# Eight second-layer modulation blocks moved from the attention stage to the first part of the RWKV mixer

## The chip, the cores and the metric

The kernel runs on one core of a Trainium2 chip. The metric is the time of one execution on the device, in microseconds (us). The time of the kernel before is the median of three runs. Beside it stands one profiled execution, whose trace gives every duration and wait that is used below. A change of 0.5%, which is 11.4 us here, is about what a measurement of this kernel can tell from no change.

## What is computed

Two layers of a diffusion backbone work on 512 latent tokens and 256 context tokens of width 1024. Layer 0 mixes the tokens with grouped-query attention, layer 1 with a two-directional RWKV-7 recurrence, and a dense SwiGLU follows each. All of it is modulated: six vectors of 1024 per layer (shift, scale and gate, for the mixer and for the SwiGLU) come from the conditioning vector `c` for the latents and from `c_ctx` for the context.

```python
for i in range(DEPTH):                                   # two layers
    m  = (silu(c)     @ mod_w[i] + mod_b[i]).reshape(B, 6, 1, D)
    mc = (silu(c_ctx) @ mod_w[i] + mod_b[i]).reshape(6, D)
    h  = rmsnorm(x,  norm1_g[i]) * (1 + m[:, 1]) + m[:, 0]
    hc = rmsnorm(xc, norm1_g[i]) * (1 + mc[1])   + mc[0]
    y, yc = attention(h, hc) if i == 0 else rwkv7(h, hc)
    x  = x + m[:, 2] * y
    h2 = rmsnorm(x, norm2_g[i]) * (1 + m[:, 4]) + m[:, 3]
    x  = x + m[:, 5] * swiglu(h2)
    ...                                                  # the context likewise, in layer 0 only
return rmsnorm(x, final_g)
```

`mod_w[i]` is a float32 matrix of 1024 x 6144. Of layer 1's six vectors only `m[:, 0]` and `m[:, 1]` (and `mc[0]`, `mc[1]`) are wanted at the RWKV mixer's entry. `m[:, 2]` is first wanted after the scan, at the output projection, and `m[:, 3]` to `m[:, 5]` later still.

## The kernel before

Activations lie with the model width on the 128 partitions: `xT[p, k, t]` holds feature 128 k + p of token t, for eight values of k and 768 tokens. Most products split both float32 operands into a high and a low float32r part and take three matmuls for the one product.

**A modulation block.** `mod_block` (L117 to L138) computes 512 of the 6144 columns for both conditioning vectors at once; a layer has twelve blocks, j = 0 to 11, two for each of the six vectors. It loads its weights, 1024 x 512 float32 or 2 MB, into tiles `mw`; eight float32 matmuls follow, one for each 128 rows. They use 32 columns of the array each, so row block k goes to column quarter k mod 4, and four of them are issued in a row. ScalarE copies the result out of PSUM (`mev`, L128), four small matmuls against `sel` add the quarters and bring the features to the partitions (L131), and VectorE adds the bias into `modT` (L132). `mod_scale` (L139 on) makes `aT`, the scale times the norm's gain, from `modT` and `par1`. The inputs of all blocks, `sc` (the silu of `c` and `c_ctx`) and `par1` (biases and gains), are in a pool that is closed when layer 0's SwiGLU opens its own.

**Stages, in the order of the trace.** Loading, norm and the first four blocks of layer 0 end at about 60 us; the q, k, v projections run to about 176 us. Then comes attention: the program lists twenty blocks (j = 4 to 23, that is the rest of layer 0 and all of layer 1) ahead of the loop over heads, each block with two weight tiles of 1 MB from two buffers. The loop over eight pairs of heads follows, for the latents first and then for the context; for each tile of 128 queries there are score matmuls `S` (L728), a maximum on VectorE (L731), an exponential on ScalarE (L735), transposes `PTp` (L742) with copies out, and for each pair the products `po` (L747). Next are the output projection and the SwiGLU of layer 0 (L228, L395, L445), whose end is layer 1's norm (`norm_stream`, L521 and L522).

The first part of the RWKV mixer starts there, at about 1026 us. `shift` builds `xx`; `lerp` builds eight tiles of `u + xx * mix[j]` on VectorE (`lt`, L897), casts them on ScalarE (`lh`, L899) and subtracts on VectorE or GpSimd (`ll`, L901), in a ring of 13 tiles; `dense(2, ...)` is the k projection, four column groups b whose weights `wraw` come in four loads of 256 KB each (L217), are cast to `whi` and subtracted to `wlo`. `sink_k` stores each result and sums squares through a tile `kq` into `ssk` (L936). Three narrow products (`rwkv_w1`, `rwkv_g1`, `rwkv_a1`) follow with a lerp each, then the normalisation of k (L991, L993, whose output `kkt` also takes the `kq` buffers), the lerp for v, and stores of the lerp for r (`d_rl`). The v projection (L1220 to L1222) and the scan come after.

**What sets the order.** The program is written for a framework that sets all semaphores and reorders: at compile time a planner runs through the program with planned durations and gives each engine's queue its order. Earlier lines of the program go first where several instructions are ready; an instruction that isn't ready lets later ones pass. On the chip each queue then runs in the planned order, and an instruction that has to wait holds up all behind it on its queue. Nearly all loads and stores are issued by SP, so SP's queue is one such order.

Of the kernel before, what the change touches and what calls it, by code (L numbers as in the profile page):

```python
# [10 lines left out]
F32 = mybir.dt.float32  # L11
# [6 lines left out]
P = 128  # L18
D = 1024
KT = D // P  # L20
L = 512
C = 256
T = L + C
# [14 lines left out]
def tile_hybrid_backbone(ctx: ExitStack, tc: tile.TileContext, a: dict, out: bass.AP, dbg=None, stop=None, start=None):  # L38
# [33 lines left out]
    with tc.tile_pool(name="prm", bufs=1, side="right", reuse_waits="tile") as prm, \  # L72
            tc.tile_pool(name="prm_ps", bufs=1, space=PSUM, reuse_waits="tile") as pps:
        rawc = prm.tile([2 * KT, P], F32, name="rawc")
        nc.scalar.dma_start(out=rawc[0:KT], in_=a["c"].rearrange("l (r p) -> (l r) p", p=P))
        nc.scalar.dma_start(out=rawc[KT:2 * KT], in_=a["c_ctx"].rearrange("(r p) -> r p", p=P))
        ps = pps.tile([P, P], F32, name="psc", tag="ps")
        nc.tensor.transpose(ps[:, 0:2 * KT], rawc, ident[0:2 * KT, 0:2 * KT])
        nc.gpsimd.memset(sc, 0.0)
        for s in range(2):  # L80
            nc.scalar.activation(sc[:, :, s], ps[:, 8 * s:8 * s + 8], AF.Silu)
        raw1 = prm.tile([P, P], F32, name="raw1")
        row = 0
        for name, n in (("mod_b", 96), ("norm1_g", 16), ("norm2_g", 16)):
            nc.scalar.dma_start(out=raw1[row:row + n, :], in_=a[name].rearrange("l (r p) -> (l r) p", p=P))
            row += n
        ps = pps.tile([P, P], F32, name="ps1", tag="ps")
        nc.tensor.transpose(ps, raw1, ident)
        nc.vector.tensor_copy(par1, ps)

    def mixer_params(prm, pps, tag):
        raw2 = prm.tile([96 + 8, P], F32, name="raw2")
# [17 lines left out]
        nc.vector.tensor_copy(par2, ps[:, 0:row])  # L110
        nc.vector.tensor_copy(ln.rearrange("p x f -> p (x f)"), ps[:, 256:256 + 2 * KT])

    modb = par1[:, 0:96].rearrange("p (l j) -> p l j", l=2)
    norm_g = par1[:, 96:128].rearrange("p (w l f) -> p w l f", w=2, l=2)


    def mod_block(pool, pspool, l, j, bufs=2, npc=2, tags=("aux", "aux"), pbufs=None):  # L117
        ps = pspool.tile([P, 512], F32, name="mps", tag=tags[0], bufs=pbufs)
        v = a["mod_w"][l].rearrange("(k p) f -> p k f", p=P)[:, :, 512 * j:512 * (j + 1)]
        nk = KT // npc  # L120
        for i in range(npc):
            w = pool.tile([P, nk, 512], F32, name="mw", tag="mw", bufs=bufs)
            nc.sync.dma_start(out=w, in_=v[:, nk * i:nk * i + nk, :])
            for k in range(nk * i, nk * i + nk):
                g = k % 4
                nc.tensor.matmul(ps[32 * g:32 * g + 32, :], sc[:, k, :], w[:, k - nk * i, :], start=(k < 4), stop=(k >= 4))  # L126
        ev = pool.tile([P, 512], F32, name="mev", tag="mev", bufs=1)
        nc.scalar.copy(ev, ps)  # L128
        ps2 = pspool.tile([P, 512], F32, name="mps2", tag=tags[1], bufs=pbufs if tags[0] == tags[1] else None)
        for q in range(4):  # L130
            nc.tensor.matmul(ps2[:, 2 * q:2 * q + 2], ev[:, 128 * q:128 * q + 128], sel, start=True, stop=True)  # L131
        nc.vector.tensor_tensor(  # L132
            out=modT[:, l, 4 * j:4 * j + 4, :],
            in0=ps2[:, 0:8].rearrange("p (q s) -> p q s", s=2),
            in1=modb[:, l, 4 * j:4 * j + 4].unsqueeze(2).to_broadcast([P, 4, 2]),
            op=ALU.add,
        )

    def mod_scale(l, w, half):  # L139
        m = (1, 4)[w]  # L140
        ks = slice(4 * half, 4 * half + 4)
        nc.vector.scalar_tensor_tensor(
            out=aT[:, 2 * l + w, ks],
            in0=modT[:, l, 8 * m + 4 * half:8 * m + 4 * half + 4, :],
            scalar=1.0,
            in1=norm_g[:, w, l, ks].unsqueeze(2).to_broadcast([P, 4, 2]),
            op0=ALU.add,
            op1=ALU.mult,
        )
# [375 lines left out]
    def layer0():  # L525
# [168 lines left out]
        with ExitStack() as sm:  # L694
# [3 lines left out]
            pst = pool(sm, "pst", 2, psum=True)  # L698
            pso = pool(sm, "pso", 1, psum=True)
            psa = pool(sm, "psa", 1, psum=True)  # L700
            for j in range(4, 24):
                mod_block(md, psa, j // 12, j % 12)

            ready = {}
            for b in range(2):
                raw = md.tile([P, KT, 256], F32, name="mw", tag="mw", bufs=2)
                nc.sync.dma_start(out=raw, in_=a["attn_wo"][0].rearrange("(k p) f -> p k f", p=P)[:, :, 256 * b:256 * b + 256])
                ready[b] = [raw[:, 0:4], raw[:, 4:8]]
            for l, w in ((0, 1), (1, 0), (1, 1)):
                for half in range(2):  # L710
                    mod_scale(l, w, half)
            tap("modT", modT[:, 0])
# [73 lines left out]
    else:  # L786
        xTs[0] = pool(xs, "xT").tile([P, KT, T], F32, name="xT")
        nc.sync.dma_start(out=xTs[0], in_=a["x0"])
        with ExitStack() as ms:
            md = pool(ms, "md")  # L790
            pam = pool(ms, "pam", 2, psum=True)
            mixer_params(md, pam, "aux")
            for j in range(12):
                mod_block(md, pam, 1, j)
            for w in range(2):
                for half in range(2):
                    mod_scale(1, w, half)
            for s, _, _ in ORDERED:
                norm_stream(s, md, pam.tile([P, 512], F32, name="rbc", tag="aux"))
        mods.close()  # L800
# [9 lines left out]
    with ExitStack() as rw:  # L810
# [37 lines left out]
        with ExitStack() as de:  # L848
# [13 lines left out]
            hkk = up.tile([P, KT], F32, name="hkk")  # L862
            xx = pool(de, "xxp").tile([P, KT, T], F32, name="xx")
            pk = pool(de, "pk", 1, psum=True)


            def shift(k, s, off, w):
# [68 lines left out]
                    nc.tensor.matmul(ssk[:, i, f, :], sq[:, P * i:P * i + P], h2, start=True, stop=True)  # L936

            dense(2, 1, T, sink_k, True)

            hbf = ep.tile([P, T], F32, name="hb", tag="lt")[:, 0:384]  # L940
            hb = hbf.rearrange("p (f h) -> p f h", f=KT)
# [545 lines left out]
```

## Time and profile before

| | |
|---|---|
| median of three runs | 2289.47 us (2286.93 to 2295.59) |
| profiled execution | 2281.48 us, of which the trace spans 2279.8 us |
| PE busy | 2024.0 us, 89% of the span |
| DVE busy | 1694.4 us, 74% |
| ACT busy | 1128.5 us, 49% |
| POOL busy | 787.6 us, 35% |
| granted TensorE clock, mean | 0.93 |
| loads of `mod_w` | 48 of 1024 KB, 5.3 us from issue to landing |

The profiled execution is one run. It is 8.0 us shorter than the median and 5.5 us shorter than the fastest of the three, so a difference between two profiles isn't the difference of two medians. PE is TensorE's matmuls and PEld its weight loads, DVE is VectorE, ACT ScalarE, POOL GpSimd and SP the queue that issues DMAs. A busy share is a mean over all stages; what a stage is limited by is read in the stage. "Granted clock" is the share of full speed that TensorE was given.

### The profile page before, as it was taken

What the parts mean: (1) busy time and instruction counts of PE and PEld (TensorE: products, weight loads), DVE (VectorE), ACT (ScalarE), POOL (GpSimd) and SP (SyncE); (2) the same over time, 40 slices, a digit from 0 to 9 for tenths busy, and PEclk for the clock granted to TensorE, in tenths of its full rate; (3) what the DMA queues carried; (4) which work ended last, traced back from release to release, by engine and by line L of the source; (5) the groups of instructions that cost most, each with busy time, mean ns of one, the idle gap of its engine ahead of it and who ended that gap; (6) DMA issues with size and microseconds to landing.
All of it is one profiled execution on the core that took longest, in us unless ns stands there. A gap on an engine that the chain in (4) does not pass through costs nothing.

```text
span 2279.8 us, 43273 instructions
## 1 busy us (share of the span) xinstructions
PE 2024.0 (89%) x16566; PEld 1785.4 (78%) x16566; DVE 1694.4 (74%) x3439; ACT 1128.5 (49%) x2338; POOL 787.6 (35%) x642
## 2 busy tenths in 40 slices
PE   6999999898999999994988877778778777999998
PEld 4995555797999999994858855667667667899998
DVE  4565555669677777669385598799787778899997
ACT  5446566655333333336243754765654556444443
POOL 1110000136444344413142532543330325666661
PEclk8999999999999999997978988878888978999999
DMA  8206772443222221211344543433321654433332
GB/s 301 67 22 221 236 234 73 147 149 137 68 61 70 74 75 56 74 54 59 101 153 153 161 132 107 116 85 94 91 59 32 187 179 120 147 99 96 111 94 74
DMA packets 196445, 260.56 MB, mean 114 GB/s; under 512 B 17384, under 2 KB 129232, under 8 KB 195856
## 3 DMA queue, kind: packets, MB, share of 16 engines
q1 hardware_dynamic: 195520, 256.95, 36.2%
q8 instruction: 131, 2.15, 0.4%
q10 hardware_dynamic: 352, 0.60, 0.1%
q14 instruction: 74, 0.61, 0.1%
q0 software_dynamic: 368, 0.26, 0.1%
HBM read 211.62 MB, written 33.55 MB: 108 GB/s over the span
## 4 chain that ended last, share of the span: by engine, by line
PE 63%; DVE 21%; DMA 5%; ACT 4%; issue 4%; POOL 2%; SPq 0%; DVEq 0%; POOLq 0%; ACTq 0%
PE yps L445 13%; PE A L395 8%; PE B L395 5%; PE C L395 5%; PE yps L228 5%; DVE O L1167 3%; PE po L747 3%; PE S L728 2%; PE pj L228 2%; DVE E L1170 2%; PE PTp L742 2%; PE mps L126 2%; PE qps L595 2%; PE qps L597 2%; PE qps L596 2%
## 5 line engine op out<-in xcount | busy, mean ns | idle before, releaser
L445 PE MATMUL yps<-gh,wu 128*128 128x384 f32 (+2 forms) x1120 | 324.4, 345 | 0.0
L258 DVE SCALAR_TENSOR_TENSOR xT<-yps,modT,xT 128x384 f32<-128x384 f32 (+3 forms) x360 | 185.2, 537 | 124.7 <-PE yps L445 105.9
L239 ACT CAST wu<-wr 128x512 fp32r<-128x512 f32 x276 | 168.5, 619 | 171.6 <-PE A L395 56.6
L239 ACT CAST wu<-ws 128x512 fp32r<-128x512 f32 x176 | 109.1, 621 | 222.6 <-PE yps L445 66.4
L445 PEld LDWEIGHTS yps<-gh,wu 128*128 128x128 f32 x1120 | 202.7, 189 | 11.4
L241 POOL TENSOR_TENSOR wu<-wr,wu 128x512 fp32r<-128x512 f32 x86 | 123.8, 1439 | 241.2 <-ACT wu L239 217.6
L445 PE MATMUL yps<-gl,wu 128*128 128x384 f32 (+2 forms) x560 | 193.2, 345 | 0.0
L349 POOL TENSOR_TENSOR ws<-wr 128x512 f32<-128x512 f32 x88 | 130.0, 1482 | 141.8 <-DMA wr<-in_ffn_wg_dram 56.4
L241 DVE TENSOR_TENSOR wu<-wr,wu 128x512 fp32r<-128x512 f32 x190 | 161.8, 857 | 12.9 <-ACT wu L239 12.4
L241 DVE TENSOR_TENSOR wu<-ws,wu 128x512 fp32r<-128x512 f32 x111 | 135.5, 1221 | 22.2 <-ACT wu L239 22.0
L241 POOL TENSOR_TENSOR wu<-ws,wu 128x512 fp32r<-128x512 f32 x65 | 100.1, 1540 | 66.1 <-ACT wu L239 65.9
L228 PE MATMUL yps<-oTh,wu 128*128 128x384 f32 (+1 forms) x512 | 110.9, 309 | 1.1 <-ACT wu L239 1.0
L445 PEld LDWEIGHTS yps<-gl,wu 128*128 128x128 f32 x560 | 105.8, 189 | 4.3
L731 DVE TENSOR_REDUCE mx<-S 128x1 f32<-128x768 f32 (+1 forms) x96 | 74.7, 778 | 44.2 <-PE S L728 43.6
L395 PE MATMUL C<-x5h,wu 128*128 128x384 f32 (+1 forms) x352 | 85.0, 319 | 14.5 <-ACT x5h L312 12.3
L743 ACT COPY PT<-PTp 128x384 f32<-128x384 f32 (+1 forms) x160 | 69.4, 466 | 53.8 <-PE PTp L742 53.6
L241 POOL TENSOR_TENSOR wu<-mw,wu 128x512 fp32r<-128x512 f32 x2 | 2.9, 1458 | 263.9 <-ACT wu L239 263.9
L742 PEld LDWEIGHTS PTp<-ident,pr 128*128 128x128 f32 x448 | 50.2, 144 | 50.4 <-issue 23.6
L1167 DVE TENSOR_TENSOR O<-E 128x110 f32<-128x110 f32 (+22 forms) x288 | 87.9, 341 | 2.2
L395 PE MATMUL A<-x1h,wu 128*128 128x384 f32 (+1 forms) x352 | 83.1, 311 | 4.5 <-POOL wu L241 2.1
L228 PEld LDWEIGHTS yps<-oTh,wu 128*128 128x128 f32 x512 | 85.4, 189 | 1.9 <-ACT wu L239 1.4
L395 PE MATMUL B<-x2h,wu 128*128 128x384 f32 (+1 forms) x352 | 84.5, 309 | 0.2 <-POOL wu L241 0.2
(409 smaller groups left out, 6482.7 us busy)
## 6 DMA issues: line engine op xcount, KB each, us to landing
mw<-in_mod_w_dram SPq DMA_DIRECT2D x48, 1024.0 KB, 5.3
wr<-in_ffn_wg_dram SPq DMA_DIRECT2D x44, 512.0 KB, 4.1
wr<-in_ffn_wu_dram SPq DMA_DIRECT2D x44, 512.0 KB, 3.8
wr<-in_ffn_wd_dram SPq DMA_DIRECT2D x44, 512.0 KB, 3.9
wraw<-in_rwkv_wrkv_dram SPq DMA_DIRECT2D x32, 256.0 KB, 3.2
wr<-in_rwkv_wo_dram SPq DMA_DIRECT2D x16, 512.0 KB, 4.7
wraw<-in_attn_wqkv_dram SPq DMA_DIRECT2D x12, 512.0 KB, 4.8
xT<-xd SPq DMA_DIRECT2D x2, 3072.0 KB, 11.0
```

The source lines that it names most:

```text
L228: nc.tensor.matmul(ps, w(k), x(k, sl), start=(k == 0 and i == 0), stop=(k == nk - 1 and i == 2))
L239: nc.scalar.copy(hi, raw)
L241: (nc.gpsimd if lane["n"] % 3 == 0 else nc.vector).tensor_tensor(out=lo, in0=raw, in1=hi, op=ALU.subtract)
L258: nc.vector.scalar_tensor_tensor(out=xT[:, f, t0:t1], in0=ps[:, t0 - sl.start:t1 - sl.start], scalar=modT[:, l, 8 * m + f, s:s + 1], in1=x ...
L349: nc.gpsimd.tensor_tensor(out=t, in0=x, in1=y, op=op)
L395: nc.tensor.matmul(ps, w[:, k], x[:, k], start=(k + j == 0), stop=(k == 3 and j == 2))
L445: nc.tensor.matmul(ps, u[k // 2][w][:, k % 2, fs], gs[k // 2][x][:, k % 2, sl], start=(k + j == 0), stop=(k == nk - 1 and j == 2))
L731: nc.vector.tensor_reduce(out=mx, in_=S[:, :nk * P], axis=AX.X, op=ALU.max)
L742: nc.tensor.transpose(ps[:, t - t0, :], pr_[:, P * t:P * t + P], ident)
L743: nc.scalar.copy(PT[h][:, t0:t1, P * qt:P * qt + P], ps[:, :t1 - t0, :])
L747: nc.tensor.matmul(po[HD * h:HD * h + HD, :], vt[:, k0 // P + t, HD * kv:HD * kv + HD], PT[h][:, t, :], start=(t == 0), stop=(t == nk - 1))
L1167: nc.vector.tensor_tensor(out=tv, in0=E[:, a_:b, s:s + 1].to_broadcast([P, b - a_, m]), in1=E[:, s:s + 1, :s].to_broadcast([P, b - a_, m]) ...
```

## The change

Blocks j = 4 to 11 of layer 1, and the `mod_scale` of its second norm, are no longer listed before the loop over heads. They are listed behind `dense(2, 1, T, sink_k, True)` in the RWKV mixer. As the tiles `sc` and `par1` are gone by then, both are stored to DRAM at the start (two DMAs issued by ScalarE) and loaded again (two DMAs issued by SP). The moved blocks load their weights in eight pieces of 256 KB, one for each 128 rows, from three buffers in the pool `nm`; they use two PSUM banks of their own (`pm`) and a `kq` buffer for `mev`. The other twelve blocks of the attention stage stay as they are.

```diff
+    d_sc = dram.tile([P, KT, 32], F32, name="d_sc")
+    d_par = dram.tile([P, P], F32, name="d_par")
+    nc.scalar.dma_start(out=d_sc, in_=sc)
+    nc.scalar.dma_start(out=d_par, in_=par1)
...
-    def mod_block(pool, pspool, l, j, bufs=2, npc=2, tags=("aux", "aux"), pbufs=None):
+    mod_in = {"sc": sc, "par": par1}
+
+    def mod_block(pool, pspool, l, j, bufs=2, npc=2, tags=("aux", "aux"), pbufs=None, ev=None):
+        sc = mod_in["sc"]
+        modb = mod_in["par"][:, 0:96].rearrange("p (l j) -> p l j", l=2)
...
-        ev = pool.tile([P, 512], F32, name="mev", tag="mev", bufs=1)
+        ev = (ev or (lambda: pool.tile([P, 512], F32, name="mev", tag="mev", bufs=1)))()
...
-            for j in range(4, 24):
+            for j in range(4, 16):
                 mod_block(md, psa, j // 12, j % 12)
...
-            for l, w in ((0, 1), (1, 0), (1, 1)):
+            for l, w in ((0, 1), (1, 0)):
                 for half in range(2):
                     mod_scale(l, w, half)
...
             pk = pool(de, "pk", 1, psum=True)
+            pm = pool(de, "pm", 2, psum=True)
...
             dense(2, 1, T, sink_k, True)
+
+            sc2 = nm.tile([P, KT, 32], F32, name="sc2")
+            par2_ = nm.tile([P, P], F32, name="par1")
+            nc.sync.dma_start(out=sc2, in_=d_sc)
+            nc.sync.dma_start(out=par2_, in_=d_par)
+            mod_in.update(sc=sc2, par=par2_)
+            for j in range(4, 12):
+                mod_block(nm, pm, 1, j, bufs=3, npc=8, ev=lambda: ep.tile([P, T], F32, name="mev", tag="kq")[:, :512])
+            for half in range(2):
+                mod_scale(1, 1, half)
```

More of the change, by code (lines that the diff above doesn't have):

```diff
@@ L111, in mixer_params @@
         nc.vector.tensor_copy(ln.rearrange("p x f -> p (x f)"), ps[:, 256:256 + 2 * KT])
-    modb = par1[:, 0:96].rearrange("p (l j) -> p l j", l=2)
-    norm_g = par1[:, 96:128].rearrange("p (w l f) -> p w l f", w=2, l=2)
-    def mod_block(pool, pspool, l, j, bufs=2, npc=2, tags=("aux", "aux"), pbufs=None):
+    mod_in = {"sc": sc, "par": par1}
+    def mod_block(pool, pspool, l, j, bufs=2, npc=2, tags=("aux", "aux"), pbufs=None, ev=None):
+        sc = mod_in["sc"]
+        modb = mod_in["par"][:, 0:96].rearrange("p (l j) -> p l j", l=2)
         ps = pspool.tile([P, 512], F32, name="mps", tag=tags[0], bufs=pbufs)
@@ L140, in mod_scale @@
         m = (1, 4)[w]
+        norm_g = mod_in["par"][:, 96:128].rearrange("p (w l f) -> p w l f", w=2, l=2)
         ks = slice(4 * half, 4 * half + 4)
@@ L792, in tile_hybrid_backbone @@
             mixer_params(md, pam, "aux")
-            for j in range(12):
+            for j in range(4):
                 mod_block(md, pam, 1, j)
-            for w in range(2):
-                for half in range(2):
-                    mod_scale(1, w, half)
+            for half in range(2):
+                mod_scale(1, 0, half)
             for s, _, _ in ORDERED:
@@ L938, in tile_hybrid_backbone @@
             dense(2, 1, T, sink_k, True)
+            sc2 = nm.tile([P, KT, 32], F32, name="sc2")
[5 more added lines that the diff above has]
+                mod_block(nm, pm, 1, j, bufs=3, npc=8, ev=lambda: ep.tile([P, T], F32, name="mev", tag="kq")[:, :512])
+            for half in range(2):
+                mod_scale(1, 1, half)
             hbf = ep.tile([P, T], F32, name="hb", tag="lt")[:, 0:384]
```

## The prediction

> **What bounds the kernel now.** I read the busy times and the chain by line first, on the page, and then the chain within the attention stage alone.
>
> ```profile
> PE 2024.0 (89%) x16566; PEld 1785.4 (78%) x16566; DVE 1694.4 (74%) x3439; ACT 1128.5 (49%) x2338; POOL 787.6 (35%) x642
> PE yps L445 13%; PE A L395 8%; PE B L395 5%; PE C L395 5%; PE yps L228 5%; DVE O L1167 3%; PE po L747 3%; PE S L728 2%; PE pj L228 2%; DVE E L1170 2%; PE PTp L742 2%; PE mps L126 2%; PE qps L595 2%; PE qps L597 2%; PE qps L596 2%
> by line: PE po L747 24.2%; PE PTp L742 23.8%; PE S L728 21.4%; PE mps L126 21.2%; PE mps L131 8.8%; ACT pr L735 0.5%; ACT PT L743 0.3%; issue 0.0%
> ```
>
> The third line is the chain from 200 to 360 us. The blocks' matmuls (L126, L131) are 30% of it, and everything else in it is matmul too: attention is limited by PE, and the blocks are on its path. How much they take is read from windows that each begin at a pair's `po`, which is one pair of heads per row (span, then PE, PEld, DVE, ACT, POOL busy; clock, DMA share, GB/s):
>
> ```profile
> 204.63:231.86 27.23, 27.23 (x181) 15.42 (x177) 13.80 (x38) 15.84 (x35) 0.00 (x0) 1.00 0.69 231
> ...
> 313.58:340.82 27.24, 27.24 (x178) 15.46 (x177) 14.72 (x38) 16.25 (x37) 0.00 (x0) 1.00 0.71 233
> 340.82:364.65 23.83, 23.68 (x146) 14.17 (x145) 14.16 (x35) 15.17 (x36) 0.00 (x0) 1.00 0.56 182
> 364.65:382.99 18.34, 17.82 (x97) 10.50 (x96) 12.28 (x34) 12.63 (x33) 0.00 (x0) 1.00 0.00 0
> ```
>
> Five pairs take 27.24 us each with PE busy throughout; the last row holds no block and takes 18.34. The same windows for L126 and then for L131 alone (weight loads) tell how many blocks lie in them:
>
> ```profile
> 204.63:231.86 27.23, 0.94 (x48) 1.00 0.69 231
> 340.82:364.65 23.83, 0.47 (x24) 1.00 0.56 182
> ...
> 204.63:231.86 27.23, 2.92 (x24) 1.00 0.69 231
> 340.82:364.65 23.83, 1.95 (x16) 1.00 0.56 182
> ```
>
> At 16 records of L126 and 8 of L131 a block, a full pair carries three. Now the part that receives the blocks, in seven windows from the norm to the scan's start:
>
> ```profile
> 1026.55:1042.84 16.29, 3.80 (x22) 3.42 (x22) 15.61 (x44) 12.00 (x24) 6.53 (x12) 0.58 0.28 97
> 1042.84:1060.75 17.91, 10.58 (x47) 9.69 (x48) 16.93 (x30) 11.09 (x23) 11.04 (x8) 0.52 0.18 59
> 1060.75:1079.99 19.24, 12.84 (x52) 8.68 (x50) 17.85 (x25) 9.72 (x16) 0.86 (x5) 1.00 0.01 1
> 1079.99:1142.97 62.98, 61.15 (x372) 54.70 (x373) 21.76 (x26) 17.15 (x24) 9.17 (x5) 0.97 0.32 101
> 1142.97:1168.00 25.03, 20.77 (x103) 15.37 (x102) 21.82 (x26) 13.97 (x21) 8.67 (x7) 0.89 0.23 67
> 1168.00:1197.00 29.00, 23.29 (x66) 15.46 (x64) 25.92 (x22) 11.05 (x14) 14.33 (x8) 0.56 0.75 245
> 1197.00:1240.00 43.00, 35.75 (x249) 34.22 (x249) 22.14 (x26) 12.93 (x27) 9.13 (x10) 0.86 0.55 177
> ```
>
> It is three different stages. Norm and first lerps (to 1080 us) are limited by VectorE, 50.4 of 53.4 us, and PE has gaps. The k projection (1080 to 1143) is PE's, 61.15 of 62.98. From 1143 to 1197 VectorE is busy 47.7 of 54 us, and PE runs partly at half clock.
>
> **The change part by part.** *Out of attention.* The step from one PE group to the next gives a block's price:
>
> ```profile
> 332.38 1.07 PE L126 MATMUL mps<-mw,sc 128*32 128x512 f32 x8
> 333.38 0.87 PE L742 MATMUL PTp<-ident,pr 128*128 128x128 f32 x6
> ...
> 337.35 0.95 PE L131 MATMUL mps<-sel,mev 128*128 128x2 f32 x8
> 338.15 0.85 PE L742 MATMUL PTp<-ident,pr 128*128 128x128 f32 x6
> ...
> 200.00:360.00 160.00, 53.29 (x416) 22.89 (x416) 2.85 (x18) 10.61 (x18) 1.00 0.71 236
> ```
>
> Half a block holds PE for 1.00 us and its gather for 0.80, so a block is 2 x 1.00 + 0.80 = 2.80 us. By the chain it is 30% of 160 us for 18 blocks (the last row is that window for the tile `mps`, with 18 bias additions on DVE), 2.67; by the windows (27.24 - 18.34) / 3 = 2.97, though the last window has shorter context scores in it, and the pair at 340.82, less one and a half blocks of L126 and two of L131 (4.6 us), leaves 19.2, which makes (27.24 - 19.2) / 3 = 2.68. I take 2.78: 8 x 2.78 = 22.2 us less, between 21.4 and 23.7. Nothing else there becomes late: ACT's busiest pair is 16.25 and DVE's 14.72, both under 18.34.
>
> *At the start* two stores are issued on ACT's queue. An issue on SP costs 0.37 us (first row below), taken for ACT's also: 0.7 us. The store of `par1` must wait for its copy on DVE, and what is queued behind it on ACT, the squares of the input, waits with it. If the order puts it early, that is up to the 7.5 us that DVE itself waits there; I take 0.7, as the plan orders by readiness.
>
> ```profile
> L123 SPq DMA_DIRECT2D mw<-in_mod_w_dram x48: 367/368/2626, 5.8 to 348.1; - x48
> DVE par L89 <- PE ps L88: 7.5, 1, 7.5
> L128 ACT COPY mev<-mps x24: 563/587/598, 22.8 to 355.0; 128x512 f32<-128x512 f32 x24
> L132 DVE TENSOR_TENSOR modT<-mps,par x24: 148/156/167, 26.2 to 357.3; 128x8 f32<-128x8 f32 x24
> L142 DVE SCALAR_TENSOR_TENSOR aT<-modT,par x8: 152/166/169, 36.3 to 338.7; 128x8 f32<-128x8 f32 x8
> ...
> 1178.66 1.01 DVE L993 SCALAR_TENSOR_TENSOR kkt<-kt,hkk,pj 128x768 f32<-128x768 f32 x1 [0.32 <-PE pj L991]
> L998 DVE SCALAR_TENSOR_TENSOR lt<-xx,par,xT x8: 739/746/751, 1207.5 to 1225.0; 128x512 f32<-128x512 f32 x8
> ```
>
> *VectorE in the mixer*: 8 x 0.156 + 2 x 0.166 = 1.6 us, on the engine that limits two of the three stages. All of it counts: +1.6. *ScalarE*: 8 x 0.587 = 4.7 us. It has room in every window, but the lerps pass through it (`lt`, `lh`), and a copy that is running cannot be put off: a third counts, +1.5, between 0 and 4.7. The copies take `kq` buffers that the squares and `kkt` use too; `kkt` is 1.01 us of work in several, so this costs nothing while the ring turns, and a copy's length each time if not.
>
> *PE in the mixer.* A half block is cheap because four column quarters run at once. A piece of one row block that arrives alone has no partner. What a pass of 512 columns takes when few share is shown by `po`, whose halves load weights in pairs (start, us):
>
> ```profile
> 205.11 0.14 PEld L747 LDWEIGHTS po<-PT,vt 128*64 128x64 f32 x2 [0.28 <-issue]
> 205.54 0.14 PEld L747 LDWEIGHTS po<-PT,vt 128*64 128x64 f32 x2 [0.28 <-issue]
> ```
>
> 0.43 us a pass, two passes a float32 matmul: 0.86 us for a lone piece. The 64 pieces and eight gathers are 64 x 0.86 + 6.4 = 61.4 us if all are alone; three buffers let three share at best, 64 / 3 x 1.00 + 6.4 = 27.7. PE's gaps are 53.4 - 27.2 = 26.2 us up to 1080, 54.0 - 44.1 = 10.0 from 1143 to 1197 and 7.2 after, 43.5 in all. The middle of 27.7 and 61.4, 44.6, just fits. In between, from 1080 to 1143, there is no room, but the dense matmuls are earlier lines and go first; I count five lone pieces that slip in, +4, between 0 and the whole overflow, 61.4 - 43.5 = 17.9. Behind 1143 the blocks are the earlier lines and hold up the narrow products; VectorE has `kkt` and the `d_rl` tiles (L998, which stood at the end) to do meanwhile, 8 x 1.01 and 8 x 0.746 us. That is the cover, and without it the products' delay is the overflow just named.
>
> *SP and the weights.* The pieces pass SP's queue, 66 issues more, amid `wraw`, `d_k` and `kt`. A piece's issue waits until PE is done with the piece three before; a `wraw` load behind it waits too, then `whi`, `wlo` and the products. These stops exist already (total, times, longest; the three stages in turn):
>
> ```profile
> ACT whi L218 <- DMA wraw<-in_rwkv_wrkv_dram: 3.8, 3, 1.8
> ...
> ACT whi L218 <- DMA wraw<-in_rwkv_wrkv_dram: 5.2, 2, 3.5
> ...
> ACT whi L218 <- DMA wraw<-in_rwkv_wrkv_dram: 5.8, 4, 4.5
> ...
> wraw<-in_rwkv_wrkv_dram SPq DMA_DIRECT2D x30, 256.0 KB, 3.4
> ```
>
> A load of this size lands in 3.4 us, and two weight buffers cover most of it: +2.5, less than one landing, between 0 and 20 (six late loads). Three in flight in 3.4 us is 231 GB/s, and the first three windows move at most 97, so the wires have room. At that pace 64 pieces take 64 / 3 x 3.4 = 73 us, longer than the 53 to 1080: some three blocks fall behind 1143.
>
> The Trainium skill, DMA: Bandwidth & Descriptors (Rules for kernel authors), speaks against the edit: at least 1 MiB per DMA, where these are a quarter. Its fixed cost of 2.0 us plus bytes over 436 GB/s (Anatomy of one DMA, for GpSimd's path) would be an estimate of 2.6 us a piece, 55 us for all, and fewer blocks behind 1143; the 3.4 us measured decides.
>
> *The clock.* From 1168 to 1185 the chain is PE at 0.56 of its clock. First and last of its four stretches of `pj` (30 matmuls, 10.3 us), one of four `L991` steps (3.7 us in all), and the same matmuls at full clock:
>
> ```profile
> 1101.56 8.44 PE pj L228 x48
> ...
> 1168.04 3.84 PE pj L228 x12
> ...
> 1180.84 0.94 PE pj L991 x2
> 1181.78 2.22 PE pj L228 x6
> ```
>
> At 8.44 / 48 = 0.176 us the 30 would be 5.3 us, so 5.0 less, and half of the `L991` steps 1.9: up to 6.9 us back if the blocks keep PE awake there, nothing if they are over by then. I take 3.0. The Trainium skill, TensorE: Matmul & The Clock Gate (What's actually happening), says that activity releases the throttle; the trace agrees (0.52 and 0.56 where PE has gaps, 1.00 in attention), and by that rule alone the term would be the whole 6.9 and the sum 3.9 us lower.
>
> *Memory.* `nm` grows by 7.5 KB a partition (`sc2` 1, `par1` 0.5, three pieces of 2), so `xx` moves and waits for other tiles of the SwiGLU. Nothing, as `xx` needs the norm anyway; a late tile would cost what it is late.
>
> *Sum*: -22.2 + 0.7 + 1.6 + 1.5 + 4 + 2.5 - 3.0 = -14.9 us. The profiled execution, 2281.48, would be 2266.6; that execution lies 8.0 under the median, so the same difference goes on the median: 2289.47 - 14.9 = 2274.6, faster by 0.65%, with 2262 to 2283 as this case's own range. A measurement tells 0.5%, 11.4 us, from no change.
>
> **The rivals.** *No change to measure*: the pieces come one by one, each takes its 0.86 us, PE becomes the limit of the whole receiving part, and the clock gains nothing as the chain moves elsewhere. Then the PE term is 17.9: -22.2 + 0.7 + 1.6 + 1.5 + 17.9 + 2.5 = +2.0, or 2291.5. For it: one load per row block and only three buffers. Against it: the gaps at half clock would widen with a waking clock.
>
> *Slower*: SP's queue. Every `wraw` load that stands behind a piece that waits for PE comes one landing late and passes it on. Without the 2.5 the sum is -17.4; each late load on the path adds 3.4, five cancel the gain, and from nine on the kernel is measurably slower. Ten give +16.6: 2306. For it: nine such stops exist, and 30 of these loads lie between 1020 and 1240. Against it: double buffers, and in attention, with the same in-order queue, no matmul of the third chain line waits for a load.
>
> *Attention doesn't give it back*, because scores, exponential and transposes become the chain: half the gain, -11.1 + 7.3 = -3.8, 2285.7. The window without a block, 17.82 of 18.34 busy, speaks against it.
>
> **How the numbers follow.** Forecast 0.57, no change 0.24, slower 0.15, attention 0.04. Of the forecast's 0.57 some 0.50 lies below 2278.1, and of the no-change case 0.02: faster 0.52. Same: 0.07 + 0.20 + 0.04 = 0.31 with 0.01 of the SP case, 0.32 in all. Slower: 0.14 + 0.02 = 0.16. The range goes from 2261 (everything hidden, and the clock's 6.9) to 2299, which takes in the no-change case and the SP case up to eight late loads.
>
> **What would show it.** In the profile after: twelve blocks' L126 in attention and first pairs still at 27.2 us, later ones at 18.3 to 19.2, and the stage's end 21 to 24 us sooner; L126 records between 1005 and 1170 us of the new time, in groups of two or three; the three windows to the k projection's start longer by 2 to 4 us together; that projection by about 4; a clock above 0.56 in the narrow products. Wrong would be: long waits of PE for `mw`, longer waits of `whi` for `wraw`, L126 in the middle of the k projection, or pairs without a block that stay above 20 us.

## The result

The changed kernel takes 2322.24 us (2314.05 to 2329.09, four runs) beside 2290.34 for the kernel before: a ratio of 1.0146 (95% interval 1.0113 to 1.0180), 32 us slower. The forecast was 2274.6, faster. The profiled execution of after is 2314.05 us with a span of 2312.2, of before 2281.48 and 2279.8, so the two traces differ by 32.4 us, about as the medians do (31.9).

The busy times of the page (this is after) differ little from those of before, by 25 us for PE and less than 10 for the others, and don't tell where the 32 us went:

```profile
PE 2049.3 (89%) x16566; PEld 1776.0 (77%) x16566; DVE 1688.1 (73%) x3439; ACT 1127.3 (49%) x2338; POOL 787.0 (34%) x642
```

So I set marks: the first or last start of a line that both kernels have (times in us from the span's start).

| | before | after |
|---|---|---|
| first score matmul `S` | 175.9 | 181.5 |
| last `po` of attention | 427.9 | 413.9 |
| last `ssk`, the k projection's end | 1146.5 | 1130.1 |
| last block's copy `mev` | 355.0 | 1236.3 |
| first `kkt` | 1172.8 | 1226.8 |
| first to last v product `pv` | 1196.2 to 1295.8 | 1238.5 to 1328.1 |
| first `z`, the scan's front | 1235.4 | 1265.8 |
| span | 2279.8 | 2312.2 |

The start lost 5.6 us. From the first `S` to the last `po` 19.6 were won, and 2.4 more up to the k projection's end, where after was 16.4 ahead. From there to the last v product it took 198.0 us where before took 149.3: 48.7 lost in one stage. Behind it both need 984 us.

Attention did nearly what was forecast. These are windows from `po` to `po` of after (span; PE, PEld, DVE, ACT, POOL busy; clock, DMA share, GB/s):

```profile
210.23:237.46 27.23, 27.23 (x181) 15.42 (x177) 13.80 (x38) 15.84 (x35) 0.00 (x0) 1.00 0.69 236
...
264.70:291.65 26.95, 26.31 (x169) 15.30 (x168) 14.73 (x38) 15.96 (x37) 0.00 (x0) 1.00 0.70 235
291.65:311.32 19.67, 19.36 (x106) 12.04 (x105) 13.81 (x33) 13.96 (x34) 0.00 (x0) 1.00 0.02 6
```

A pair without blocks takes 19.67, so a block is (27.23 - 19.67) / 3 = 2.5 us and eight are 20.2.

Where the 48.7 went, by the chain of after from 1130 to 1240 us, and by what each engine waited for from 1130 to 1245 (total, times, longest):

```profile
by line: PE mps L131 31.8%; DMA mw<-in_mod_w_dram 30.8%; PE pj L234 21.3%; PE mps L136 8.4%; ACT mev L133 2.7%; issue 1.3%; PE pj L1007 1.0%; PE rnp L999 0.7%; PE pv L1236 0.6%; PE pv L1237 0.4%; PE ssk L942 0.4%; SPq L128 0.4%; PE pv L1238
...
PEld mps L131 <- DMA mw<-in_mod_w_dram: 44.5, 32, 3.9
ACT mev L133 <- PE mps L131: 40.9, 7, 12.4
...
ACT whi L224 <- DMA wraw<-in_rwkv_wrkv_dram: 9.0, 5, 3.0
```

The blocks (L131, L136, L133) and their loads are three quarters of the chain. TensorE's weight loads wait 44.5 us for pieces; `whi` waits 9.0 for `wraw`. The blocks' matmuls alone, in windows (PE, PEld busy):

```profile
1011.00:1065.70 54.70, 6.75 (x16) 0.80 (x16) 0.81 0.33 104
1065.70:1130.10 64.40, 0.00 (x0) 0.00 (x0) 0.97 0.32 104
1130.10:1170.00 39.90, 13.62 (x36) 1.82 (x36) 1.00 0.51 146
1170.00:1190.00 20.00, 12.81 (x24) 1.65 (x24) 0.83 0.71 216
1190.00:1238.50 48.50, 26.64 (x53) 3.67 (x52) 0.79 0.72 228
```

At some 16 records a block, one block ran ahead of the k projection, none in it, seven behind it. Their copies on ScalarE, first and last of eight, with what it waited for:

```profile
1128.73 0.58 ACT L133 COPY mev<-mps 128x512 f32<-128x512 f32 x1
...
1225.01 0.59 ACT L133 COPY mev<-mps 128x512 f32<-128x512 f32 x1 [12.41 <-PE mps L131]
1236.33 0.59 ACT L133 COPY mev<-mps 128x512 f32<-128x512 f32 x1 [10.74 <-PE mps L131]
```

From the first to the last it takes 107.6 us for seven blocks, 15.4 each; the last, with hardly anything beside it, 11.3, which is 1.4 a piece. And this is its end, from the timeline:

```profile
1230.50 1.69 PE L131 MATMUL mps<-mw,sc 128*32 128x512 f32 x4 [1.72 <-DMA mw<-in_mod_w_dram]
...
1234.38 1.86 PE L131 MATMUL mps<-mw,sc 128*32 128x512 f32 x4 [0.93 <-DMA mw<-in_mod_w_dram]
...
1236.97 0.97 PEld L136 LDWEIGHTS mps<-sel,mev 128*128 128x128 f32 x8 [1.64 <-ACT mev L133]
...
1237.95 0.62 PE L1007 MATMUL pj<-rn,hsel 48*128 48x512 f32 x2
...
1238.50 0.39 PE L1236 MATMUL pv<-whi,lh 128*128 128x256 f32 x1
```

The v products begin in the microsecond in which the last block's gather (L136) is done, and the trace shows no wait of theirs for an operand. The scan's front waits too. Its first tiles are set by GpSimd, and one of them, `wa`, is released by `kkt`, which comes late (waits from 1130 to 1270):

```profile
POOL wa L1034 <- DVE kkt L1009: 43.6, 1, 43.6
```

That is the picture to be explained: who makes the blocks so slow, and why does so much wait for the last of them?

### The profile page after: what moved, and what is told of

It is laid out like the page before. It is cut to its first block, busy times and chain, and to the rows that moved or that the text cites. A ratio compares the mean times of both kernels' runs of the same rounds, so it can differ in the third digit from the quotient of the medians.

```text
span 2312.2 us, 43374 instructions
## 1 busy us (share of the span) xinstructions
PE 2049.3 (89%) x16566; PEld 1776.0 (77%) x16566; DVE 1688.1 (73%) x3439; ACT 1127.3 (49%) x2338; POOL 787.0 (34%) x642
## 4 chain that ended last, share of the span: by engine, by line
PE 61%; DVE 18%; DMA 7%; ACT 6%; issue 4%; POOL 3%; SPq 0%; DVEq 0%; ACTq 0%; POOLq 0%
PE yps L451 11%; PE A L401 6%; PE B L401 5%; PE C L401 4%; PE yps L234 4%; PE pj L234 3%; PE mps L131 3%; PE po L753 3%; PE S L734 2%; DVE wu L247 2%; DVE O L1183 2%; PE PTp L748 2%; PE pr L1347 2%; DVE E L1186 2%; DMA mw<-in_mod_w_dram 2%
## 5 line engine op out<-in xcount | busy, mean ns | idle before, releaser
L247 DVE TENSOR_TENSOR wu<-ws,wu 128x512 fp32r<-128x512 f32 x111 | 137.9, 1243 | 21.5 <-ACT wu L245 21.2
L131 PE MATMUL mps<-mw,sc 128*32 128x512 f32 x384 | 97.9, 697 | 16.4 <-DMA mw<-in_mod_w_dram 16.3
L401 PE MATMUL B<-x7h,wu 128*128 128x384 f32 (+1 forms) x352 | 83.1, 314 | 0.3 <-POOL wu L247 0.3
```

The costliest lines, as they stand in the source:

```text
L247: (nc.gpsimd if lane["n"] % 3 == 0 else nc.vector).tensor_tensor(out=lo, in0=raw, in1=hi, op=ALU.subtract)
L401: nc.tensor.matmul(ps, w[:, k], x[:, k], start=(k + j == 0), stop=(k == 3 and j == 2))
```

## The experiments

The first theory had three prices: the ring of three pieces (its round), `mev` in the `kq` ring, and the store of `par1` at the start. Each ratio below is to runs of the kernel before in the same set (medians 2286.1 to 2289.0).

**e1, no blocks at all** behind the k projection; the rest of the change stays:

```diff
-            for j in range(4, 12):
-                mod_block(nm, pm, 1, j, ...)
...
+            nc.vector.memset(modT[:, 1, 16:48], 0.0)
...
```

> Leaves the eight moved blocks out altogether (the twelve by eight values of modT that they make are set to zero, and the second scale of layer 1 too); the two stores and the two loads stay. Theory (the blocks themselves, held back to the end of the k projection and then run as a chain of loads, cost the loss): attention gives 19.6 us, layer 0's SwiGLU 2, the start costs 5.5, and the stage after the k projection is back at its old length: 2290 - 16 = 2274 us. Rival (the 7.5 KB shift of the tiles or another order of the rest makes the stage longer, not the blocks): still above 2300 us.

Measured: 2263.43, ratio 0.9897 (0.9872 to 0.9923). That is 59 us under after by the medians and 50 by the traces (2262.5 against 2312.2; after's profiled execution was its shortest of four), and 11 under what was expected. Up to the last `po` the two traces agree within 0.8 us, so all of it lies in the receiving part: without blocks the v products run from 1183.7 to 1277.4, and the stage from the last `ssk` on takes 143.1 us, 6 less than before.

**e2, the store of `par1` issued by GpSimd.**

```diff
-    nc.scalar.dma_start(out=d_par, in_=par1)
+    nc.gpsimd.dma_start(out=d_par, in_=par1)
```

> The changed kernel, with the store of par1 issued by GpSimd instead of ScalarE. Theory (ScalarE's queue stands 5 us at that store, which waits for the first mod_w load on its counting semaphore, and the last square, the norm and the copies stand behind): the first score matmul comes 5 to 6 us sooner and the kernel takes about 2317 us. Rival (the start is limited by the loads that arrive, and the wait only shows where): 2322 us and the first score matmul where it is.

Measured: 2313.60, ratio 1.0122 (1.0087 to 1.0156); first `S` at 176.4, as before. The store's price is 5 to 6 us in the traces; the intervals of e2 and of after overlap. ScalarE's timeline of after shows it:

```profile
12.37 0.19 ACT L493 ACTIVATION_READ_ACCUMULATOR sq<-xin 128x1 f32 x1
17.42 0.35 ACTq L93 DMA_DIRECT2D d_par<-par  x1
17.87 1.06 ACT L493 ACTIVATE sq<-xin 128x1024 f32<-128x1024 f32 x1 [5.32 <-DMA mw<-in_mod_w_dram]
```

The last square stands behind the store's issue; by its releaser the issue waited for a load of `mw`, not for `par1`, which was copied at 10.64. In the compiled program the issue waits for a semaphore that it shares with that load.

**e3, `mev` in the ring of the pieces** instead of a `kq` buffer.

```diff
-mod_block(nm, pm, 1, j, bufs=3, npc=8, ev=lambda: ep.tile([P, T], F32, name="mev", tag="kq")[:, :512])
+mod_block(nm, pm, 1, j, bufs=3, npc=8, ev=lambda: nm.tile([P, 512], F32, name="mev", tag="mw", bufs=3))
```

> The changed kernel, with mev in the ring of the three weight pieces instead of a kq buffer; nothing else. Theory (kq: the first copy waits for the squares of the whole k projection, so one block of eight runs before it): three blocks run before the k projection, the stage behind it is shorter by two blocks or more at 11.5 us each, 23 to 35 us, and the kernel takes 2287 to 2299 us. Rival (kq only shows the wait; the three-piece ring and its loads pace all eight anyway): 2315 to 2322 us.

Measured: 2308.57, ratio 1.0095 (1.0067 to 1.0122), between the two; in the traces it is only 1.6 us shorter than after. More blocks now run ahead of the k projection, whose last `ssk` moves from 1130 to 1150. In the chain from 1015 to 1150 us the blocks' matmuls (L131) have some 18 us and waits for pieces some 6; in after's chain from 1015 to 1130 neither appears.

```profile
by line: PE pj L234 50.2%; PE mps L131 13.1%; PE ssk L942 8.3%; DMA mw<-in_mod_w_dram 4.1%; DMA wraw<-in_rwkv_wrkv_dram 3.0%; DVE xx L875 2.9%; DVE xT L527 2.7%; ACT xT L528 2.3%; issue 2.2%; DVE wlo L225 2.0%; PE mps L136 1.9%; DVE ll L907
```

The last block still ends at 1239.5. So `kq` did hold the blocks back (in after the first `mev` of a moved block starts at 1128.73, right behind the last square at 1127.93), but freeing it moves the waiting more than it removes it.

**e4, two pieces in the ring** (`bufs=2` where after has `bufs=3`).

> The changed kernel with two weight pieces in flight instead of three. Theory (behind the k projection each round of the ring is a landing of some 3 us and an issue and a matmul, 4.2 us for three pieces): 2.1 instead of 1.4 us a piece, for some 35 pieces that run in an open chain: 25 us more, 2347 us. Rival (the pace is set by PE, a piece alone taking 0.86 us, and by the other work that shares it): within 5 us of 2322.

Measured: 2365.93, ratio 1.0345 (1.0300 to 1.0391). It is 44 us over after, where 25 were expected: the theory's direction, and its size missed. The ring's round sets the pace: 54 pieces issued behind the k projection take 144 us (1133 to 1277), 2.7 each, where after took 105 for 53, 2.0 each, and the waits from 1133 to 1282 grow with it:

```profile
ACT mev L133 <- PE mps L131: 81.7, 7, 20.9
PEld mps L131 <- DMA mw<-in_mod_w_dram: 79.7, 40, 5.7
```

The bytes don't set it: from 1190 to 1238 us this kernel moves 174 GB/s, after 230 and e9 (below) 289.

**e5, pieces of four row blocks by 128 columns**, so that the four column quarters run at once.

```diff
...
+w = pool.tile([P, 4, 128], F32, name="mw", tag="mw", bufs=bufs)
+nc.sync.dma_start(out=w, in_=v[:, h:h + 4, 128 * c:128 * c + 128])
+for g in range(4):
+    nc.tensor.matmul(ps[32 * g:32 * g + 32, 128 * c:128 * c + 128], sc[:, h + g, :], w[:, g, :], ...)
...
```

> A piece of 256 KB now holds four row blocks of 128 columns (512-byte rows) instead of one row block of 512 columns; its four matmuls go to the four column quarters and can run together. Everything else as after. Theory (the ring's round sets the pace behind the k projection: landing 3.0 us, issue 0.4, matmul 1.04, divided by three buffers, 1.45 us a piece): only the matmul's part shrinks, from 1.04 to some 0.3 to 0.4 us, so a piece takes 1.24 us, the 53 pieces behind 1130 us end some 11 to 12 us sooner, and the time is about 2310 (2302 to 2316). Rival (the price is TensorE's work, 59.8 us of lone pieces, as in the prediction's no-change case): that work falls to some 22 us, and the time with it by about 35: 2280 to 2290.

Measured: 2319.15, ratio 1.0145 (1.0116 to 1.0175): no change from after. The blocks' L131 from 1011 us on is the first row for after, the second for e5 (L132 there; PE, PEld busy):

```profile
1011.00:1240.00 229.00, 59.82 (x128) 7.94 (x128) 0.89 0.47 146
```

```profile
1011.00:1245.00 234.00, 35.03 (x512) 14.52 (x512) 0.76 0.48 146
```

25 us of TensorE's work went, and the time did not move. In after, with one block ahead of the k projection, TensorE's work for the blocks isn't the price. The 11 us that I expected of the ring did not come either; a landing took 3.5 us here instead of 3.0 in after, which can account for most of them (0.5 us over three buffers and 53 pieces is 9), though no run shows that alone.

**e9, one load for all pieces**: the moved blocks load one piece and use it 64 times; 63 loads are left out, and the blocks' results are others.

> As after, but the moved blocks load one piece only, and all their 64 pieces of work use it (63 loads of 256 KB are left out, so modT's part is another; matmuls, copies, kq buffers, PSUM banks, gathers and stores stay). Theory (what costs is the round of the three buffers: a piece's landing, behind which TensorE's queue stands): nothing is left to wait for, the blocks run as fast as in attention, 2.8 us each, seven of them behind 1130 us beside the narrow products, and the v products begin at about 1190 us as without the blocks; e1's 2263 and 8 to 20 us of the blocks' own work: 2270 to 2284. Rival (the kq buffers that keep seven blocks behind the k projection, or TensorE's work, are the price by themselves): 2300 or more.

Measured: 2266.21, ratio 0.9908 (0.9876 to 0.9939), 3 us above e1 and better than expected. `kq`, the two banks, copies, gathers and stores are all still there; the blocks end at 1184.8. (The matmuls run four at a time here and hold TensorE 18.0 us, but by e5 that is not what counts.) The 56 us between e9 and after (48 by the traces) hang on the 63 loads.

**e6, e3 with the blocks listed behind the stores of the lerp for r.**

> As e3 (mev in the ring of pieces), with the eight blocks listed behind the stores of the lerp for r, so that narrow products and the normalisation of k come first on TensorE where both are ready; the v products stay behind the blocks in the program. Theory (the blocks are held by their ring and, as earlier lines, hold up the narrow products and the v products): against e3, kkt ends some 20 us sooner and the v products begin as the blocks let them; if the v products can pass the blocks, the time is 2285 to 2297, if not about 2300. Rival (order does not matter, the blocks' TensorE work or the bytes are the price): as e3, 2305 to 2312.

Measured: 2317.54, ratio 1.0134 (1.0108 to 1.0160), 9 us longer than e3 and outside what either side expected: the list's order did not help. `kkt` was through at 1209, but the v products began at 1240.0, again behind the last block (1238.4).

**e7, e5 with e3 and e2.**

> e5, e3 and e2 together: pieces of four row blocks, mev in the ring of pieces, and the store of par1 issued by GpSimd. Theory (three separate prices: the store at the start 6 to 8 us, mev's buffer 14, the matmul's part of the ring's round 11): 2322 less 32, about 2290 (2284 to 2296), still not faster than before because the ring's landing stays. Rival (TensorE's lone pieces are the price): 2322 - 14 - 8 - 35, about 2265.

Measured: 2301.99, ratio 1.0054 (1.0031 to 1.0077), 6 us over the theory's range and far over the rival's: the three prices don't add up. Blocks end at 1226.3, v products begin at 1228.7. From the last `po` to the last `ssk` it takes 726 us, e3 735 and after 716, so ahead of the k projection, other than behind it, the pieces of e5 are worth some 9 us.

In all kernels with eight loaded blocks so far the first v product came 1.6 to 3.4 us behind the start of the last `mev`. A cause may lie in the allocation. No view of the profile shows PSUM banks; in the compiled program the first tile of `pv` is in PSUM bank 5, which in the kernel before was free, and which the change gives to the blocks' `mps`. In the planned order of TensorE's queue that matmul waits on TensorE itself, in the kernel before only on ScalarE's `whi`. e10 and e11 test it.

**e10, e7 with the blocks listed late, and e11, the same with other banks**: the pool `pd` is split in two so that `pm` gets banks 3 and 4, which only the scan wants; the tiles of `pd` use the two parts in turn.

```diff
-            pd = pool(de, "pd", 2, psum=True)
+            pds = [pool(de, "pd", 1, psum=True)]
...
             pk = pool(de, "pk", 1, psum=True)
             pm = pool(de, "pm", 2, psum=True)
+            pds.append(pool(de, "pd1", 1, psum=True))
```

> e7 with the eight blocks listed behind the stores of the lerp for r. It is the partner of e11. In both theories as e7 or a little longer, as e6 was 9 us longer than e3: 2300 to 2312; the v products begin 2 to 5 us behind the last block, as in all kernels with blocks so far.

> e10 with another layout of PSUM alone: the blocks' two banks are those that the scan wants last, so that the first tile of the v products (which in after lies in the bank of the blocks' mps) no longer waits for the last block. In the order of TensorE's queue some 11 of the 64 pieces then stand behind the first v product, before none. Theory (the bank is what ties the v products to the last block): the v products begin some 11 x 1.3 = 14 us earlier against the last block, and the time is 8 to 14 us under e10: 2288 to 2300. Rival (TensorE's queue and the ring hold everything anyway, the bank costs nothing of its own): as e10.

Measured: e10 2313.83, ratio 1.0107 (1.0081 to 1.0134); e11 2289.84, ratio 1.0010 (0.9992 to 1.0028): 24 us for the layout of PSUM alone, more than expected. Weight loads of `pv`, e10 and then e11:

```profile
L1242 PEld LDWEIGHTS pv<-whi,lh x192: 187/192/333, 1238.6 to 1327.3; 128*128 128x128 f32 x192
```

```profile
L1249 PEld LDWEIGHTS pv<-whi,lh x192: 186/192/330, 1205.6 to 1302.7; 128*128 128x128 f32 x192
```

In e11 the v products begin 27 us ahead of the last block's copy (1232.2).

**e13, after with the layout of PSUM changed alone**: `pm` opened ahead of `pk`, and `pv` with two banks, ssk's and the free one.

> After, with the layout of PSUM changed alone: the blocks' pool is opened ahead of ssk's, and the v products get two banks (ssk's and the free one) in place of three, none of them the blocks'. In the plan of TensorE's queue some 28 of the 64 pieces then stand behind the first v product; in after all 64 stand ahead of it. Theory (the bank that the first v product shares with the blocks' mps is what puts the ring's round on the path): the v products begin at 1195 to 1215 us instead of 1238 and the rest of the blocks runs between them; TensorE's work from 1130 to the last v product is 178 us in after, with 20 us idle, so 15 to 20 us less: 2298 to 2307. Rival (e11's gain came from the late listing or the pieces of four row blocks): as after, 2318 to 2326, or longer for want of the third bank.

Measured: 2324.85, ratio 1.0161 (1.0136 to 1.0185): no gain, as the rival said, but not by its mechanism. The v products did begin 57 us sooner and were through 33 us sooner, at 1294.7. What came late instead is `kkt` and the scan's front (first and last start of each):

```profile
L1009 DVE SCALAR_TENSOR_TENSOR kkt<-kt,hkk,pj x8: 1003/1012/1017, 1254.9 to 1293.3; 128x768 f32<-128x768 f32 x8
...
L1067 PE MATMUL z<-t,wa x96: 377/483/796, 1306.2 to 1692.2; 128*128 128x256 f32 x96
```

In after `z` began at 1265.8 and ended at 1682.7. Two things end together just ahead of the front here. With the early list, `kkt` (through L1007) stands behind the blocks in TensorE's queue; the last one starts at 1293.3. And a clearing of `Pb`, a tile of the scan, stands ahead of the front's tiles on GpSimd's queue in this kernel alone, and waits for the last v product (timeline of GpSimd, with the wait):

```profile
1295.13 0.96 POOL L1249 MEMSET Pb<- 128x1024 f32 x1 [100.99 <-PE pv L1238]
1296.01 1.81 POOL L1034 MEMSET Xs<- 128x2048 f32 x1
```

The last `kkt` and the last v product end 1 us apart, so e13 doesn't tell which of them costs the front its time. That `kkt` can hold it is shown by the wait of `wa` in after, 43.6 us, and e3 is the reverse case: there `kkt` was through at 1224 and `z` began at 1249, while the v products still stood behind the last block. So there are two followers of the last block: the v products through a PSUM bank, and the scan's front, by these waits through `kkt` or `modT`, which I take to hold the memory it needs. Freeing one leaves the other.

**e16, both ties loosened for all eight blocks**: e10 (late list, four row blocks, GpSimd's store) with e13's layout.

> All eight blocks with pieces of four row blocks, mev in the ring, the store of par1 by GpSimd, listed behind the stores of the lerp for r (e10), and e13's layout. In the plan 24 of the 64 pieces stand ahead of the first v product and the rest between the v products and the first inversions. Theory (with banks of its own and lone pieces that hold TensorE 0.4 us instead of 1.0 the ring's round is hidden beside 90 us of v products): the v products begin near 1190 and take 90 + some 20: 2262 to 2280, faster than before. Rival (TensorE's queue, in order, still stands at every late piece; 3.5 us for each of some 40): 2290 or more, as e11.

Measured: 2282.63, ratio 0.9964 (0.9951 to 0.9977), against the 2313.83 of e10, between what theory and rival expected. The v products run from 1178.2 to 1279.1, as without blocks. What is left is the scan's front: `z` starts at 1252.1, where e1 has 1220.0, and a tile of the front waits for the last block:

```profile
POOL eU L1044 <- DVE modT L144: 29.3, 1, 29.3
```

**Fewer blocks.** e8 moves only blocks 8 to 11, with e3's and e2's edits. e12 has pieces of four row blocks, `mev` in `kq`, GpSimd's store and e11's banks. e14 is e12 with after's banks, e15 e14 with e13's. e17 is after with four blocks for eight and nothing else changed. e18 is e16 with six.

```diff
-            for j in range(4, 12):
+            for j in range(8, 12):
```

> Only blocks 8 to 11 are moved (4 to 7 stay in the attention stage), mev in the ring, the store of par1 by GpSimd, pieces as in after. Theory (the ring's pace, 36 tiles at 1.45 us, 52 us; some 15 to 20 of them end before the k projection, the rest by about 1160 us, before the narrow products are due): attention gives back 4 x 2.6 = 10 us, the receiving part costs 2 to 8: 2281 to 2290. Rival (each lone piece costs its 1.0 us of TensorE beyond what the gaps take): 32 - 10 of gaps - 10, 2296 to 2304.

> Four blocks moved (8 to 11) with pieces of four row blocks, mev in a kq buffer as in after, the store of par1 by GpSimd and the blocks' own PSUM banks of e11. Theory (e8's loss is in the stretch ahead of the k projection, where blocks that are not held by kq slip in and TensorE's queue waits for their pieces; with kq only one block and three pieces fit there and cost nothing, as in after; the other three need about 29 tiles x 1.3 = 38 us behind 1130, beside 50 us of narrow products): attention gives 10 back, the rest costs 0 to 5: 2276 to 2284, the first to beat the kernel before. Rival (four blocks cost the same however they are laid out): as e8, 2290 to 2296.

> e12 with the layout of PSUM of after: the first v product waits for the blocks' mps again (the four blocks ended at 1190 us in e12) and no longer for the last pj of the normalisation (1219 us in e12). Theory (e12 lost what it had because its layout tied the v products to that normalisation): the v products begin at 1192 to 1200, 89 us of them and 984 behind: 2265 to 2278. Rival (four blocks cost the same however they are laid out): as e12 and e8, 2290 to 2296.

> e14 with e13's layout: the v products wait neither for the blocks nor for the normalisation. Theory: as e14 or up to 5 us less, 2262 to 2276; two banks in place of three cost the v products nothing as long as ScalarE copies a bank out (0.64 us) inside a bank's 2.8 us of matmuls. Rival: as e12, 2290 to 2296, or above e14 for want of the third bank.

> After, with one size changed: blocks 8 to 11 are moved instead of 4 to 11, everything else (pieces of one row block, mev in kq, store of par1 by ScalarE, layout of PSUM) as in after. Theory (the time follows the end of the last block: the v products through PSUM, the scan's front through the first part's memory): three blocks behind the k projection instead of seven, at 11.5 to 14 us each, end at about 1190 to 1200 with the attention 10 us longer; v products from there, 89 us, and 984 behind: 2270 to 2284, faster than before although the start's 5.6 us stay. Rival (e14 is faster because of its pieces of four row blocks and its store by GpSimd): 2290 to 2300.

> e16 with six blocks moved (6 to 11) instead of eight. In e16 the v products were through at 1279, but the scan's front began at 1247, where e14 had it at 1233, as its memory waits for the last modT. Theory (that wait is what e16 lost): the last block ends some 25 us sooner, at about 1220, the scan's front begins by 1233, attention costs 5 us more than in e16: 2264 to 2276, as e14 and e15. Rival (TensorE's own work for the blocks is what e16 lost): half way between e15 and e16, 2275, or more.

| | us | ratio (interval) | last `ssk` | last `mev` | `pv` | first `z` |
|---|---|---|---|---|---|---|
| e8 | 2293.59 | 1.0040 (1.0019 to 1.0060) | 1155.6 | 1162.4 | 1205.7 to 1303.0 | 1246.4 |
| e12 | 2294.72 | 1.0034 (1.0021 to 1.0048) | 1140.6 | 1190.4 | 1219.8 to 1308.7 | 1235.3 |
| e14 | 2268.49 | 0.9901 (0.9878 to 0.9923) | 1141.4 | 1189.6 | 1193.0 to 1285.8 | 1239.6 |
| e15 | 2267.21 | 0.9895 (0.9875 to 0.9914) | 1140.9 | 1192.3 | 1185.9 to 1285.9 | 1238.7 |
| e17 | 2287.78 | 0.9999 (0.9982 to 1.0016) | 1148.7 | 1199.6 | 1201.8 to 1297.3 | 1248.1 |
| e18 | 2271.43 | 0.9930 (0.9913 to 0.9946) | 1135.7 | 1201.2 | 1184.1 to 1284.4 | 1218.2 |

e8 came out between its theory and its rival. It lost ahead of the k projection: from the last `po` to the last `ssk` it takes 735 us, after 716 and e14, with `mev` in `kq` again and pieces of four row blocks, 720. e12 failed through my own layout: it put the pool of `kkt`'s `pj` where the first v product lies, which then began right behind the last `kkt` (weight loads of `pv` in e12, then in e14):

```profile
L1023 DVE SCALAR_TENSOR_TENSOR kkt<-kt,hkk,pj x8: 1000/1006/1014, 1191.4 to 1218.8; 128x768 f32<-128x768 f32 x8
...
L1250 PEld LDWEIGHTS pv<-whi,lh x192: 187/192/330, 1219.8 to 1308.6; 128*128 128x128 f32 x192
```

```profile
L1243 PEld LDWEIGHTS pv<-whi,lh x192: 186/192/330, 1193.0 to 1285.7; 128*128 128x128 f32 x192
```

Going back to after's banks gave 26 us, as e14's theory expected, and a version that beats the kernel before by 1.0% (e14); e15 is the same within the intervals. e17 shows that fewer blocks alone only level the loss: 34 us less than after, but the start's 5.6 us and a block end 10 us later than e14's stay. Both theories missed e17, from either side. e18's expected place was met, but its last `mev` came at 1201, not at 1220, so it says little on the wait for memory; six blocks are no better than four.

## Why the prediction was wrong

Its terms in turn. *Attention*, 22.2 forecast between 21.4 and 23.7; 20.2 by the pairs and 19.6 by the marks. The mechanism was right, and the size a little high, because the pair without blocks takes 19.67 where 18.34 and 19.2 had been read. *The start*, 0.7 taken, 5.6 measured, inside the bound of 7.5 that the prediction had put aside because "the plan orders by readiness"; the plan had the store ahead of the last square, and e2 took it back. *VectorE and ScalarE*, 1.6 and 1.5: not seen apart; e9, which has all of their work, is 2.8 us above e1, inside the noise of the two. *PE*, 0 to 17.9, and with it the no-change rival: e5 and e9 show that TensorE's own work for lone pieces did not set the time of after; in e3, with more blocks ahead of the k projection, it did count, some 18 us. The Trainium skill, TensorEngine Tiling (Array Packing) (Key Properties), says that different tiles can execute in parallel; e5 agrees in direction, with 35.0 us where 59.8 were, at a lower clock. *The clock*, 3 to 6.9 back: the granted clock did rise, from 0.56 (1168 to 1197 before) to 0.83 and 0.79 (1170 to 1190 and from there on), and nothing can be seen of it in the time; in e5 it was 0.50 from 1190 to 1243, and the kernel took as long. The rows that the prediction took as agreement are mixed besides: its own windows have 1.00 with PE busy 12.84 of 19.24 us, and 0.56 with 23.29 of 29.00. *SP*, 2.5 and the slower rival: `whi`'s waits for `wraw` are 9.0 us from 1130 to 1245, and were 12.6 in the same window before; that is not the mechanism, and that its 2306 lay nearest to the result was luck.

So the loss is not in attention or at the start. From the last `po` to the last v product the terms add up to +6.6 (1.6 + 1.5 + 4 + 2.5 - 3.0); the marks give +46.3 (48.7 less the 2.4 won up to the k projection's end). The step that failed is *PE in the mixer* with its cover: +4, between 0 and 17.9, for work that gaps of 43.5 us would take.

Two premises failed with it. The first is "The copies take `kq` buffers ... so this costs nothing while the ring turns": the plan gave no moved block a `kq` buffer until all eight squares were done, and `mps` and `mev` turn in program order, so one block ran ahead of the k projection where five were counted, and seven instead of "some three" fell behind it. By e3 this alone is worth some 14 us by the medians, and 2 by the traces. The second is the cover for these: "VectorE has `kkt` and the `d_rl` tiles ... to do meanwhile". `kkt` itself stood behind the blocks in TensorE's queue, and the prediction did not ask which work would next take the blocks' PSUM banks. Neither costs much without the slow pieces: e9 has the `kq` wait and the same banks and list and is as fast as no blocks, because blocks that need not wait for their loads are done by 1185. And the slow pieces cost less without the ties: e16 is e10 without the tie of the v products, with the same loads, and gains 31 us on it.

The step itself: the price was taken as work to be fitted into gaps (44.6 us, 61.4 at most, against 43.5). It was a latency: 1.4 to 1.9 us a piece, in a ring of three that each go through a landing of 3.0, an issue of 0.37, a matmul of 1.04 and the queues between them. "At that pace 64 pieces take ... 73 us" stands in the prediction, but without the stretch of 64 us in which the blocks got no turn, and without the stops of TensorE's queue. The Trainium skill, DMA: Bandwidth & Descriptors (Rules for kernel authors), with its 1 MiB per DMA, had spoken against the edit on this point. The traces agree in direction: loads of 1024 KB took 5.3 us to land before, pieces of a quarter of that 3.0 in after. No run moves the blocks with larger pieces.

Left open: why e14 is 19 us faster than e17. Their traces differ by 21.1: the start gives 4.7, the way from there to the first `z` 3.8 more, and 11.4 is in the scan, 413.6 us from first to last `z` in e17 and 402.2 in e14. The two differ in the pieces and in the issue of the store, and no run separates these. Which of `kkt` and `Pb` held the scan's front in e13 is open too. Whether the wait of e16's front for `modT` is what it loses against e15, 15 us, was not isolated either.

## What to carry to other kernels

Work moved into gaps is not only work: ask how long it lives, that is when its last instruction ends, and which buffers, PSUM banks and queue places it holds until then, and look up who takes these next. A small ring of small loads has a pace of its own, here 2.0 us a piece with three buffers and 2.7 with two, whatever the engines' room, and should not stand ahead of a critical chain in an in-order queue. When such a move fails, move less of it: four blocks with the ties checked gave 1.0% where eight cost 1.5%.

## What the runs showed of the hardware

A DMA issue on ScalarE's queue held the engine's own work for 5.3 us behind a load that had nothing to do with its data (17.42, above); the square queued behind it waited with it. Pieces of the same 256 KB landed in 3.5 us with rows of 512 bytes and in 3.0 with rows of 2 KB. With two banks instead of three under the v products e15 took as long as e14 (2267.21 and 2268.49); its v products began 7 us sooner and ended at the same time, so what the third bank is worth by itself isn't shown.
